# First block's mixers: norm chains on GpSimd, queries and keys without the row scale, one reciprocal for two softmaxes, two kinds of copies on ScalarE

## The chip, the cores and the metric

The kernel runs on one core of a Trainium2 chip. The metric is the device time of one execution in microseconds, the median of several executions. Engine names are short throughout: PE is TensorE, DVE is VectorE, ACT is ScalarE, POOL is GpSimd, SP is SyncE.

## What is computed

Two transformer blocks of two layers each, run one after the other on 512 tokens of width 1024, all in float32. The change touches only the mixer of the first block. There 16 meta tokens are put in front, so the sequence has 528 rows. Cut to what matters:

```python
for l in range(DEPTH):                       # DEPTH = 2
    hn = rms_norm(h, norm_mix_g[l])
    proj = hn @ w_in[l]                      # 1024 -> 2560
    q, k, v, xr, gate = jnp.split(proj, splits, axis=-1)
    q = apply_partial_rope(rms_norm(q, q_norm_g[l]), cos, sin)   # per head of 64
    k = apply_partial_rope(rms_norm(k, k_norm_g[l]), cos, sin)
    o_attn = diff_attention(q, k, v, lam)    # softmax(q1 k1) - lam softmax(q2 k2), times v
    o_attn = rms_norm(o_attn, subln_g[l]) * (1.0 - lam_init)     # per head of 128
    o_rec = rms_norm(rg_lru_branch(xr, gate, ...), rec_norm_g[l])  # over 512
    h = h + jnp.concatenate([o_attn, o_rec], axis=-1) @ w_out[l]
    ...                                      # norm, gated feed-forward of 2816
```

`rms_norm(x, g)` is `x * rsqrt(mean(x * x) + 1e-6) * g`.

## The kernel before

Features lie on partitions, tokens on the free dimension. Each product with a weight is done three times on PE (`mm3`, L95 to L98: high part times high part, high times low, low times high), in spans of 264 columns (two spans of 264 make 528) or, where the 16 meta rows are no longer needed, of 512. A weight tile is loaded by DMA, its high part is made by ACT (L90), its low part by DVE (L92); three of each can be in flight.

The first block's mixer runs per layer through a list of steps: the recurrent branch of four feature tiles (`r`), keys, queries and values of four head pairs (`k`, `q`, `v`), attention of a pair in two groups of rows (`a`), the gates (`g`), their norm (`R`, L545) and two passes of the output product (`w`). This list is only a priority. A scheduler of the framework lays the instructions of each engine down in a fixed order when the program is built, and interleaves the steps by what it takes each instruction to cost. On the chip every engine then works through its own order, and waits at the first instruction whose input is not there.

The norms all go through `rnorm` (L153). PE sums the squares over partitions with matmuls of two columns (L161, tile `av`). DVE turns the sums into mean plus epsilon (L164, tile `nwv`), and `rsqrt` (L128) makes 1/sqrt in eight dependent instructions on tiles of 88 x 12 or 128 x 8 numbers (L135 to L148, tiles `nwy`, `nwt`, `nwu`). For queries and keys, ACT then widens the result (L170, tile `nrep`); for the other norms PE reads it directly. PE transposes it into a PSUM bank (L176, tile `bc`), and DVE multiplies the data by it (L399 for queries and keys, L518 for the attention's output). In the text a **chain** is the part from L164 to L148.

In the two mixers there are 26 such chains outside the norms of the residual: 16 for queries and keys (`rows`, L389), 8 for the attention's output (end of `attend1`, L516), 2 for the recurrent branch (`recout`, L548).

Queries and keys come out of PSUM with a multiplication by `rbc`, the row scale of the preceding norm (L396, DVE, 28 instructions). The softmaxes of the two halves of a differential head each have a reciprocal (L489, 72 in all). The attention's output is copied from PSUM by DVE (L513, 16 instructions) and squared by ACT (L514).

Of the kernel before, what the change touches and what calls it, by code (L numbers as in the profile page):

```python
# [9 lines left out]
F32 = mybir.dt.float32  # L10
F32R = mybir.dt.float32r
BF = mybir.dt.bfloat16
I32 = mybir.dt.int32
AF = mybir.ActivationFunctionType
OP = mybir.AluOpType
AX = mybir.AxisListType

D = 1024
S = 512
NM = 16  # L20
T = S + NM
# [4 lines left out]
# columns of the first block's packed per-feature parameters  # L26
G_MIX, G_FFN, QG, KG, SUB, CW, CB, BRG, BIG, LRU, RECG, LAM = 0, 8, 16, 17, 18, 19, 35, 39, 43, 47, 51, 55
N_PAR1 = 59
# columns of the packed shape constants
# [5 lines left out]
# columns of the second block's packed per-feature parameters  # L35
# [11 lines left out]
def both_blocks(ctx: ExitStack, tc: tile.TileContext, xT, cst, par1, w1in, w1out, w1gu, w1dn, wgate,  # L47
# [6 lines left out]
    EARLY = 4  # tiles of features that the norms' first centre is taken from  # L54
# [7 lines left out]
    # ---- residual (features on partitions) and constants  # L62
# [4 lines left out]
    # the operand of most products: 8 tiles in two parts each  # L67
# [14 lines left out]
    # ---- building blocks  # L82
# [23 lines left out]
    def share(part):  # L106
        """who has the extra bank in a part of the program"""
        nonlocal extra
        extra = EXTRA[part]
# [18 lines left out]
    def rsqrt(pool, v, rows, n, between=()):  # L128
        """1/sqrt: y from half the exponent, then y (1 + a polynomial of v y^2 - 1) to the last bit"""
# [5 lines left out]
        nc.vector.tensor_scalar(y.bitcast(I32), v.bitcast(I32), -0.5, 1597463007.0, op0=OP.mult, op1=OP.add)  # L135
        next(other, None)
        nc.vector.tensor_mul(t, y, y)
        next(other, None)
        nc.vector.tensor_mul(t, t, v)
        next(other, None)  # L140
        nc.vector.tensor_scalar(t, t, -1.0, RSQRT[0], op0=OP.add, op1=OP.mult)
        next(other, None)
        nc.vector.scalar_tensor_tensor(u, t, RSQRT[1], t, op0=OP.add, op1=OP.mult)
        for c in RSQRT[2:]:
            next(other, None)
            nc.vector.scalar_tensor_tensor(u, u, c, t, op0=OP.add, op1=OP.mult)
        next(other, None)
        nc.vector.scalar_tensor_tensor(y, u, 1.0, y, op0=OP.add, op1=OP.mult)  # L148
# [4 lines left out]
    def rnorm(pool, xs, a, b, rhs, n, eps):  # L153
        """1/sqrt(the sums of xs over the partitions, as rhs groups them, / n + eps), on every partition of a group"""
        c = rhs.shape[1]
# [7 lines left out]
        v = pool.tile([128, 16], F32, name="nwv", bufs=3)  # L163
        nc.vector.tensor_scalar(v[:ch, :2 * J], ps[:ch, :2 * J], 1.0 / n, eps, op0=OP.mult, op1=OP.add)  # L164
        y = rsqrt(pool, v, ch, 2 * J)
# [25 lines left out]
    def tables():  # L191
        """rope tables of the given positions"""
# [27 lines left out]
    # ================= first block  # L220
    WOUT = ((0, 4), (4, 8))  # what the mixer's output product sums over, group by group
    # weights of the second block's mixer whose low parts GpSimd makes
    POOLW = (1, 0, 1, 0, 1, 0, 1)
    # tiles of the output product over half the tokens at a time, at its end and its start
    MIXTAIL = 3
    MIXHEAD = 0
    # steps whose weights are scaled by VectorE
    BYDVE = ('A010', 'A201', 'A211')
    # the first input products of the second block's mixer
    HEAD = (2, 3, 0)  # L230
    # pairs of tiles that a norm writes as one
    MERGED = (2, 4)
    # the order of the tiles of queries for the choice of keys
    TOPK = (2, 3, 1)
    # the order of the second block's mixer: H I Q input products, i scores of the indexer, p a part of the choice of
    # keys, d attention to the chosen ones, C and A attention in chunks (pair, head, group of rows), v convolution
    STEPS2 = ('H', 'I', 'Q0', 'i2', 'Q2', 'i1', 'i3', 'Q1', 'C0', 'd0', 'A000', 'A001', 'C1', 'A011', 'A100', 'A010', 'A101', 'p', 'A110', 'A111', 'C2', 'v0', 'p', 'd3', 'p', 'p', 'A201', 'p', 'd2', 'v1', 'A200', 'p', 'd1', 'A211', 'p', 'A210')
    # the order of the first block's mixer: r recurrent branch, k q v of a head pair, a attention (pair, group of rows),
    # g gates, R their norm, w output product
# [3 lines left out]
    for l in range(2):  # L243
# [4 lines left out]
        with ExitStack() as lay:  # L248
# [76 lines left out]
            with ExitStack() as mixer:  # L325
# [63 lines left out]
                def rows(m, gain, spans, dst):  # L389
# [5 lines left out]
                    for p, a, b in proj(w, xa, spans):  # L395
                        nc.vector.tensor_mul(raw[:, a:b], p, rbc[:, a:b])  # L396
# [826 lines left out]
```

## Time and profile before

| | |
|---|---|
| device time, median of 3 executions | 2865.7 us (2865.55 to 2867.1) |
| profiled execution, first to last instruction | 2861.2 us |
| PE busy in it | 2781.5 us, 97% |
| DVE / ACT / POOL busy | 1736.3 / 1227.4 / 367.0 us |
| stretches of the two mixers | about 30 to 255 us and 660 to 890 us |

The profiled execution's span, 2861.2 us, is what the rows further down are parts of. It is 4.5 us under the median of the three times, a share that lies around the span and is taken as constant. Matmuls are pipelined, so that PE counts as busy while one is in flight: busy time close to 100% means that no gap is longer than the pipeline, not that no time is lost.

### The profile page before, as it was taken

What the parts mean: (1) busy time and instruction counts of PE and PEld (TensorE: products, weight loads), DVE (VectorE), ACT (ScalarE), POOL (GpSimd) and SP (SyncE); (2) the same over time, 40 slices, a digit from 0 to 9 for tenths busy, and PEclk for the clock granted to TensorE, in tenths of its full rate; (3) what the DMA queues carried; (4) which work ended last, traced back from release to release, by engine and by line L of the source; (5) the groups of instructions that cost most, each with busy time, mean ns of one, the idle gap of its engine ahead of it and who ended that gap; (6) DMA issues with size and microseconds to landing.
All of it is one profiled execution on the core that took longest, in us unless ns stands there. A gap on an engine that the chain in (4) does not pass through costs nothing.

```text
span 2861.2 us, 42993 instructions
## 1 busy us (share of the span) xinstructions
PE 2781.5 (97%) x16548; PEld 2422.5 (85%) x16548; DVE 1736.3 (61%) x3534; ACT 1227.4 (43%) x2174; POOL 367.0 (13%) x403
## 2 busy tenths in 40 slices
PE   8989999999999999999999999999999999999998
PEld 7989999999887888887889888888877898888887
DVE  7887434457888434458977573333789875633335
ACT  6665222235665222235665442332445754433323
POOL 0011000000110000002220031111322110311112
PEclk9999999999999999999999999999999999999999
DMA  4332332332333333336324123333264242233331
GB/s 146 89 79 85 90 89 85 94 89 92 99 85 100 95 92 94 94 95 166 112 82 140 59 81 97 96 96 96 70 155 132 75 136 72 60 106 95 96 96 64
DMA packets 96491, 277.18 MB, mean 97 GB/s; under 512 B 13344, under 2 KB 20000, under 8 KB 96288
## 3 DMA queue, kind: packets, MB, share of 16 engines
q1 hardware_dynamic: 96288, 274.45, 32.7%
q8 instruction: 131, 2.15, 0.3%
q14 instruction: 72, 0.59, 0.1%
HBM read 241.82 MB, written 2.10 MB: 85 GB/s over the span
## 4 chain that ended last, share of the span: by engine, by line
PE 87%; DVE 8%; issue 2%; ACT 2%; POOL 1%; DMA 1%; SPq 0%; ACTq 0%; DVEq 0%; POOLq 0%
PE mm L97 25%; PE mm L98 25%; PE mm L96 25%; PE av L96 1%; PE av L97 1%; PE av L98 1%; PE av L161 1%; DVE wlo L92 1%; PE bc L827 1%; PE av L712 1%; PE tr L827 1%; DVE sq L402 1%; PE bc L176 0%; PE sc L96 0%; PE sc L833 0%
## 5 line engine op out<-in xcount | busy, mean ns | idle before, releaser
L96 PE MATMUL mm<-xh_all,whi 128*128 128x512 f32 (+2 forms) x2752 | 926.0, 338 | 12.4 <-ACT xh_all L260 6.8
L97 PE MATMUL mm<-xl_all,whi 128*128 128x512 f32 (+2 forms) x2752 | 930.3, 339 | 1.4 <-DVE xl_all L745 0.8
L98 PE MATMUL mm<-xh_all,wlo 128*128 128x512 f32 (+2 forms) x2752 | 925.9, 337 | 0.0
L90 ACT CAST whi<-wraw 128x1024 fp32r<-128x1024 f32 (+2 forms) x460 | 465.4, 1013 | 1017.7 <-PE mm L97 823.9
L92 DVE TENSOR_TENSOR wlo<-wraw,whi 128x1024 fp32r<-128x1024 f32 (+2 forms) x437 | 540.7, 1238 | 233.7 <-ACT whi L90 231.7
L96 PEld LDWEIGHTS mm<-xh_all,whi 128*128 128x128 f32 x2752 | 518.8, 189 | 66.6 <-ACT xh_all L260 6.8
L97 PEld LDWEIGHTS mm<-xl_all,whi 128*128 128x128 f32 x2752 | 519.8, 189 | 54.5 <-DVE xl_all L745 1.8
L98 PEld LDWEIGHTS mm<-xh_all,wlo 128*128 128x128 f32 x2752 | 521.0, 189 | 49.8
L1106 POOL TENSOR_TENSOR r<-r 128x512 f32<-128x512 f32 (+1 forms) x70 | 101.9, 1456 | 531.6 <-ACT r L1105 531.6
L97 PE MATMUL mm<-yl,whi 128*128 128x264 f32 (+1 forms) x528 | 169.9, 322 | 0.1
L98 PE MATMUL mm<-yh,wlo 128*128 128x264 f32 (+1 forms) x528 | 169.5, 322 | 0.0
L96 PE MATMUL mm<-yh,whi 128*128 128x264 f32 (+1 forms) x528 | 168.5, 320 | 0.0
L673 DVE TENSOR_TENSOR hall<-hall,mm 128x512 f32<-128x512 f32 (+1 forms) x82 | 46.6, 568 | 145.9 <-PE mm L98 145.9
L593 DVE TENSOR_TENSOR su<-mm,rbc 128x264 f32<-128x264 f32 (+1 forms) x66 | 34.3, 519 | 139.8 <-PE mm L98 139.8
L602 DVE TENSOR_TENSOR hall<-hall,mm 128x264 f32<-128x264 f32 (+1 forms) x72 | 37.1, 515 | 120.6 <-PE mm L98 120.6
L97 PEld LDWEIGHTS mm<-yl,whi 128*128 128x128 f32 x528 | 99.2, 188 | 8.8 <-DVE yl L122 0.6
L96 PEld LDWEIGHTS mm<-yh,whi 128*128 128x128 f32 x528 | 99.0, 188 | 7.6
L98 PEld LDWEIGHTS mm<-yh,wlo 128*128 128x128 f32 x528 | 99.2, 188 | 7.3
L588 DVE TENSOR_TENSOR sg<-mm,rbc 128x264 f32<-128x264 f32 (+1 forms) x66 | 34.0, 517 | 103.2 <-PE mm L98 101.6
L671 DVE SCALAR_TENSOR_TENSOR hall<-hall,mm 128x512 f32<-128x512 f32 x32 | 22.0, 687 | 66.9 <-PE mm L98 66.8
L692 POOL TENSOR_TENSOR accq<-accq,nsq 128x512 f32<-128x512 f32 (+1 forms) x48 | 57.9, 1205 | 25.4 <-ACT nsq L690 24.0
L432 POOL MEMSET vh<- 128x128 f32 x8 | 1.6, 205 | 463.6 <-PE mm L98 414.8
(672 smaller groups left out, 5446.3 us busy)
## 6 DMA issues: line engine op xcount, KB each, us to landing
wraw<-w2f SPq DMA_DIRECT2D x128, 512.0 KB, 3.7
wraw<-w1gu SPq DMA_DIRECT2D x88, 512.0 KB, 3.6
wraw<-w2in SPq DMA_DIRECT2D x44, 512.0 KB, 3.9
wraw<-w1in SPq DMA_DIRECT2D x40, 512.0 KB, 3.7
wraw<-w2mkv SPq DMA_DIRECT2D x32, 512.0 KB, 3.8
wraw<-w1dn SPq DMA_DIRECT2D x32, 448.0 KB, 3.3
wraw<-w1out SPq DMA_DIRECT2D x32, 256.0 KB, 2.7
wraw<-w1dn SPq DMA_DIRECT2D x16, 512.0 KB, 3.5
```

The source lines that it names most:

```text
L90: nc.scalar.copy(hi[:, :kt], raw[:, :kt])
L92: (eng or nc.vector).tensor_sub(lo[:, :kt], raw[:, :kt], f(hi[:, :kt]))
L96: nc.tensor.matmul(ps, wh, xh, start=first, stop=False)
L97: nc.tensor.matmul(ps, wh, xl, start=False, stop=False)
L98: nc.tensor.matmul(ps, wl, xh, start=False, stop=last)
L588: nc.vector.tensor_mul(sg[:, a:b], p, r2[:, a:b])
L593: nc.vector.tensor_mul(su[:, a:b], p, r2[:, a:b])
L602: nc.vector.tensor_add(h[m][:, a:b], h[m][:, a:b], p)
L673: nc.vector.tensor_add(X(m, a, b), X(m, a, b), p)
L692: nc.gpsimd.tensor_add(self.accq[:, a:b], self.accq[:, a:b], sq[:, a:b])
L827: nc.tensor.transpose(ps[:, 128 * j:128 * j + 128], p[:, 128 * j:128 * j + 128], ident)
L1106: nc.gpsimd.tensor_mul(r[:, a:b], r[:, a:b], r[:, a:b])
```

## The change

It makes five edits, all in the mixers of the first block.

1. `rsqrt` and `rnorm` take an engine. The chains of queries and keys, of the attention's output and of the recurrent norm go to POOL. [...] The first instruction (mean plus epsilon, out of PSUM) stays with DVE.
2. Queries and keys are no longer multiplied by the row scale. The norm takes the scale out anyway, if epsilon is multiplied by the mean square of the row, which `rnorm` of the preceding norm now keeps (`kept`, tile `ms`). L164 becomes a scalar_tensor_tensor there. In the second layer, four extra matmuls and two DVE instructions make `msl`, the same numbers in the token grouping that the queries use; each layer has one more DVE instruction to scale `ms`.
3. With that, the copy of queries and keys out of PSUM is a plain copy, by ACT.
4. The reciprocals of the two halves are one instruction over a stepped pair of columns.
5. The copy of the attention's output out of PSUM goes from DVE to ACT.

```diff
-    def rsqrt(pool, v, rows, n, between=()):
+    def rsqrt(pool, v, rows, n, between=(), eng=None):
+        eng = eng or nc.vector
...
-        nc.vector.scalar_tensor_tensor(u, t, RSQRT[1], t, op0=OP.add, op1=OP.mult)
+        if eng is nc.gpsimd:
+            for n, c in enumerate((*RSQRT[1:], 1.0)):
+                eng.tensor_scalar(u, u if n else t, c, None, op0=OP.add)
+                eng.tensor_mul(u if c != 1.0 else y, u, t if c != 1.0 else y)
+            return y
+        eng.scalar_tensor_tensor(u, t, RSQRT[1], t, op0=OP.add, op1=OP.mult)
...
-    def rnorm(pool, xs, a, b, rhs, n, eps):
+    def rnorm(pool, xs, a, b, rhs, n, eps, eng=None, scales=None, kept=None):
...
-        v = pool.tile([128, 16], F32, name="nwv", bufs=3)
-        nc.vector.tensor_scalar(v[:ch, :2 * J], ps[:ch, :2 * J], 1.0 / n, eps, op0=OP.mult, op1=OP.add)
-        y = rsqrt(pool, v, ch, 2 * J)
+        v = pool.tile([128, 16], F32, name="nwv", bufs=3) if kept is None else kept
+        if scales is None:
+            nc.vector.tensor_scalar(v[:ch, :2 * J], ps[:ch, :2 * J], 1.0 / n, eps, op0=OP.mult, op1=OP.add)
+        else:
+            nc.vector.scalar_tensor_tensor(v[:ch, :2 * J], ps[:ch, :2 * J], 1.0 / n, scales[:ch, :2 * J], op0=OP.mult,
+                                           op1=OP.add)
+        y = rsqrt(pool, v, ch, 2 * J, eng=eng)
...
-                rows = rnorm(small, sumsq(small, h, 0, T), 0, T, one2, D, 1e-6)
+                ss = sumsq(small, h, 0, T)
+                rows = rnorm(small, ss, 0, T, one2, D, 1e-6, kept=ms)
+                ps = bank("av")
+                for j in range(4):
+                    nc.tensor.matmul(ps[:, 2 * j:2 * j + 2], ss[0][:, l0 + 128 * j:l0 + 128 * j + 128], one2, start=True, stop=True)
+                nc.vector.tensor_scalar(msl[:, :8], ps[:, :8], 1.0 / D, 1e-6, op0=OP.mult, op1=OP.add)
+                nc.vector.tensor_scalar(msl[:, :8], msl[:, :8], 1e-6, None, op0=OP.mult)
...
+            nc.vector.tensor_scalar(ms[:88, :12], ms[:88, :12], 1e-6, None, op0=OP.mult)
...
                     for p, a, b in proj(w, xa, spans):
-                        nc.vector.tensor_mul(raw[:, a:b], p, rbc[:, a:b])
+                        nc.scalar.copy(raw[:, a:b], p)
                     nc.scalar.activation(sq[:, a0:b0], raw[:, a0:b0], AF.Square)
-                    for p, a, b in rnorm(small, [sq], a0, b0, blk, 64, 1e-6):
+                    for p, a, b in rnorm(small, [sq], a0, b0, blk, 64, 1e-6, nc.gpsimd, ms if a0 == 0 else msl):
...
-                            nc.vector.reciprocal(st[:n, o + 5:o + 6], st[:n, o + 3:o + 4])
                             pr.append(p)
+                        nc.vector.reciprocal(st[:n, 5:12:6], st[:n, 3:10:6])
...
-                    nc.vector.tensor_copy(oT[:, g0:g1], ps[:, :g])
+                    nc.scalar.copy(oT[:, g0:g1], ps[:, :g])
...
-                    for p, a, b in rnorm(small, [sq], l0, T, one2, 128, 1e-6):
+                    for p, a, b in rnorm(small, [sq], l0, T, one2, 128, 1e-6, nc.gpsimd):
...
-                    for p, a, b in rnorm(small, sums, l0, T, one2, 512, 1e-6):
+                    for p, a, b in rnorm(small, sums, l0, T, one2, 512, 1e-6, nc.gpsimd):
```

The scheduler lays the two mixers down anew on every engine; from the second block on, all five orders are as before. Two places show what moves. The names carry buffer numbers here, which differ between the programs; the line numbers of the changed program are larger by 5 to 18.

First, DVE in layer 0 at the norm of the first queries (sums `av_784` before, `av_789` after). `d` and `xc` belong to the recurrent branch, `raw_943` to the next keys. Before:

```order
L164 TENSOR_SCALAR nwv_791<-av_784 88x12
L378 TENSOR_SCALAR d_711<-d_711 128x528
L135 TENSOR_SCALAR nwy_793<-nwv_791 88x12
L356 SCALAR_TENSOR_TENSOR xc_888<-xr_834,par_81,xc_888 128x528
L137 TENSOR_TENSOR nwt_794<-nwy_793 88x12
L396 TENSOR_TENSOR raw_943<-mm_945,rbc_174 128x264
L139 TENSOR_TENSOR nwt_794<-nwt_794,nwv_791 88x12
L356 SCALAR_TENSOR_TENSOR xc_888<-xr_834,par_81,xc_888 128x528
L141 TENSOR_SCALAR nwt_794<-nwt_794 88x12
L92 TENSOR_TENSOR wlo_1156<-wraw_1152,whi_1154 128x1024
L381 TENSOR_TENSOR d_711<-d_711,ig_689 128x528
L143 SCALAR_TENSOR_TENSOR nwu_795<-nwt_794 88x12
```

After:

```order
L172 SCALAR_TENSOR_TENSOR nwv_796<-av_789,ms_115 88x12
L374 SCALAR_TENSOR_TENSOR xc_684<-xr_630,par_81,xc_684 128x528
L370 TENSOR_TENSOR xr_843<-mm_845,rbc_174 128x264
L122 TENSOR_TENSOR xcl_690<-xc_684,xch_689 128x528
L417 SCALAR_TENSOR_TENSOR raw_734<-raw_734,gs_186,bc_815 128x264
L370 TENSOR_TENSOR xr_843<-mm_870,rbc_174 128x264
L417 SCALAR_TENSOR_TENSOR raw_734<-raw_734,gs_186,bc_819 128x264
```

Before, the chain's steps stand between the recurrent branch's and a weight's, and `raw` times `bc` (L399) comes 21 instructions after L164. After, three instructions stand between L172 and the multiplication that needs the broadcast (L417). On PE at the same place, 69 matmuls of 264 columns stood between the sums and the first broadcast of this norm; now 30 do.

Second, PE in layer 0 at the recurrent branch's norm (`R`), from the sums to the first broadcast. `mm` is the gates' product, `sc` the scores of an attention tile. Before:

```order
L161 MATMUL av_2615<-one2_74,ss_acc_2130 88x2 x6
L97 MATMUL mm_3038<-rl3_2608,whi_3034 128x264
L98 MATMUL mm_3038<-rh3_2607,wlo_3036 128x264
L471 MATMUL sc_2678<-k1_1447,qs_1558 128x272
L476 MATMUL sc_2678<-k2_1448,qs_1558 128x272
L471 MATMUL sc_2682<-k1_1447,qs_1558 128x256
L474 LDWEIGHTS ident_b_76
L474 MATMUL sc_2682<-mask_b_77,ident_b_76 128x128
L476 MATMUL sc_2682<-k2_1448,qs_1558 128x256
L176 MATMUL bc_2635<-cs_68,nwy_2624 128x88 x3
```

After:

```order
L166 MATMUL av_2643<-one2_74,ss_acc_2157 88x2 x6
L98 MATMUL mm_3046<-rh3_2635,wlo_3031 128x264
L97 MATMUL mm_3071<-rl3_2636,whi_3067 128x264
L98 MATMUL mm_3071<-rh3_2635,wlo_3069 128x264
L489 MATMUL sc_2723<-k1_1463,qs_1578 128x272
L185 MATMUL bc_2667<-cs_68,nwy_2652 128x88 x3
```

Eight matmuls between sums and broadcast have become four.

## Rows read from the trace of the kernel before

**Rows 1.** The page: busy time of the engines; the chain that ended last.
```profile
PE 2781.5 (97%) x16548; PEld 2422.5 (85%) x16548; DVE 1736.3 (61%) x3534; ACT 1227.4 (43%) x2174; POOL 367.0 (13%) x403
...
PE 87%; DVE 8%; issue 2%; ACT 2%; POOL 1%; DMA 1%; SPq 0%; ACTq 0%; DVEq 0%; POOLq 0%
```

**Rows 2.** Windows: length, busy us (instructions) of each engine, clock, DMA.
```profile
30.00:255.00 225.00, 212.04 (x1694) 197.37 (x1692) 185.10 (x502) 137.40 (x275) 32.20 (x51) 0.98 0.28 77
660.00:890.00 230.00, 221.12 (x1472) 191.62 (x1472) 194.91 (x487) 138.15 (x265) 31.50 (x47) 1.00 0.31 84
300.00:350.00 50.00, 50.00 (x413) 50.00 (x412) 24.05 (x36) 14.13 (x18) 0.00 (x0) 1.00 0.30 87
950.00:1000.00 50.00, 50.00 (x218) 40.53 (x217) 22.07 (x26) 14.07 (x17) 0.00 (x0) 1.00 0.34 96
```

**Rows 3.** PE's waits, 30 to 255 us: total us, times, longest.
```profile
PE sc L471 <- ACT p L485: 3.1, 1, 3.1
PE av L161 <- ACT sq L397: 2.2, 4, 0.8
PE bc L176 <- DVE nwy L148: 2.0, 2, 1.4
```

**Rows 4.** Groups by shape, DVE: count, busy us, mean ns, idle before.
```profile
L396 DVE TENSOR_TENSOR raw<-mm,rbc 128x264 f32<-128x264 f32 x24 | 10.0, 419 | 0.5 <-PE mm L98 0.5
L489 DVE RECIPROCAL st<-st 128x1 f32<-128x1 f32 x64 | 9.6, 155 | 2.5 <-ACT p L485 2.1
L513 DVE COPY oT<-av 128x256 f32<-128x256 f32 x12 | 5.1, 421 | 4.4 <-PE av L98 4.3
L137 DVE TENSOR_TENSOR nwt<-nwy 88x12 f32<-88x12 f32 x20 | 3.2, 160 | 0.2
```

**Rows 5.** Groups by shape, ACT, 0 to 950 us.
```profile
L170 ACT COPY nrep<-nwy 88x768 f32<-88x768 f32 x12 | 9.9, 826 | 4.0 <-DVE nwy L148 4.0
L288 ACT COPY rbc<-bc 128x264 f32<-128x264 f32 x4 | 1.5, 378 | 6.5 <-PE bc L176 6.5
```

**Rows 6.** Timeline (start, length): a chain alone on DVE, then PE's broadcast.
```profile
248.57 0.17 DVE L164 TENSOR_SCALAR nwv<-av 88x12 f32<-88x12 f32 x1 [0.75 <-PE av L161]
...
250.19 0.17 DVE L148 SCALAR_TENSOR_TENSOR nwy<-nwu,nwy 88x12 f32<-88x12 f32 x1
250.41 0.44 PE L176 MATMUL bc<-cs,nwy 88*128 88x88 f32 x3
```

**Rows 7.** Timeline: the first queries' chain among other work; widening; broadcast.
```profile
72.50 0.17 DVE L164 TENSOR_SCALAR nwv<-av 88x12 f32<-88x12 f32 x1 [0.38 <-PE av L161]
...
79.92 0.83 ACT L170 COPY nrep<-nwy 88x768 f32<-88x768 f32 x1 [1.71 <-DVE nwy L148]
...
80.84 0.33 PE L176 MATMUL bc<-cs,nrep 88*128 88x88 f32 x2
```

**Rows 8.** POOL: groups by shape, then timeline rows, undisturbed.
```profile
L350 POOL MEMSET xr<- 128x3 f32 x8 | 0.8, 100 | 53.1 <-DVE xc L356 31.6 <-PE av L161 19.2 <-PE av L98 1.9
...
200.41 1.31 POOL L401 TENSOR_TENSOR raw<-raw,ct 128x528 f32<-128x528 f32 x1 [4.54 <-DVE sq L400]
208.62 0.74 POOL L559 TENSOR_TENSOR hall<-hall,raw 128x264 f32<-128x264 f32 x1 [6.90 <-DVE raw L558]
...
1493.11 1.31 POOL L692 TENSOR_TENSOR accq<-accq,nsq 128x512 f32<-128x512 f32 x1 [4.29 <-ACT nsq L690]
1494.49 1.29 POOL L692 TENSOR_TENSOR accq<-accq,nsq 128x512 f32<-128x512 f32 x1
...
1500.26 0.74 POOL L692 TENSOR_TENSOR accq<-accq,nsq 128x256 f32<-128x256 f32 x1
1500.95 0.73 POOL L682 TENSOR_TENSOR acc<-acc,hall 128x256 f32<-128x256 f32 x1
```

**Rows 9.** Timeline: POOL and DVE at the same time.
```profile
247.13 0.69 DVE L92 TENSOR_TENSOR wlo<-wraw,whi 128x512 fp32r<-128x512 f32 x1
247.20 1.22 POOL L559 TENSOR_TENSOR hall<-hall,raw 128x264 f32<-128x264 f32 x1 [0.72 <-DVE raw L558]
```

More of the change, by code (lines that the diff above doesn't have):

```diff
@@ L134, in rsqrt @@
         other = iter(between)
-        nc.vector.tensor_scalar(y.bitcast(I32), v.bitcast(I32), -0.5, 1597463007.0, op0=OP.mult, op1=OP.add)
+        eng.tensor_scalar(y.bitcast(I32), v.bitcast(I32), -0.5, 1597463007.0, op0=OP.mult, op1=OP.add)
         next(other, None)
-        nc.vector.tensor_mul(t, y, y)
+        eng.tensor_mul(t, y, y)
         next(other, None)
-        nc.vector.tensor_mul(t, t, v)
+        eng.tensor_mul(t, t, v)
         next(other, None)
-        nc.vector.tensor_scalar(t, t, -1.0, RSQRT[0], op0=OP.add, op1=OP.mult)
+        eng.tensor_scalar(t, t, -1.0, RSQRT[0], op0=OP.add, op1=OP.mult)
         next(other, None)
-        nc.vector.scalar_tensor_tensor(u, t, RSQRT[1], t, op0=OP.add, op1=OP.mult)
+        if eng is nc.gpsimd:
[4 more added lines that the diff above has]
+        eng.scalar_tensor_tensor(u, t, RSQRT[1], t, op0=OP.add, op1=OP.mult)
         for c in RSQRT[2:]:
             next(other, None)
-            nc.vector.scalar_tensor_tensor(u, u, c, t, op0=OP.add, op1=OP.mult)
+            eng.scalar_tensor_tensor(u, u, c, t, op0=OP.add, op1=OP.mult)
         next(other, None)
-        nc.vector.scalar_tensor_tensor(y, u, 1.0, y, op0=OP.add, op1=OP.mult)
+        eng.scalar_tensor_tensor(y, u, 1.0, y, op0=OP.add, op1=OP.mult)
         for _ in other:
@@ L151, in rsqrt @@
         return y
-    def rnorm(pool, xs, a, b, rhs, n, eps):
-        c = rhs.shape[1]
+    def rnorm(pool, xs, a, b, rhs, n, eps, eng=None, scales=None, kept=None):
         ch = 88 if (b - a) % 88 == 0 else 128
@@ L271, in both_blocks @@
             prep(G_MIX, 0, T)
+            ms = small.tile([128, 16], F32)
+            msl = small.tile([128, 16], F32, name="msl") if l else ms
             if l == 0:
@@ L282, in both_blocks @@
                             nc.vector.tensor_add(acc, acc, sq)
-                    rows = rnorm(small, [acc], 0, T, one2, D, 1e-6)
+                    rows = rnorm(small, [acc], 0, T, one2, D, 1e-6, kept=ms)
             else:
-                rows = rnorm(small, sumsq(small, h, 0, T), 0, T, one2, D, 1e-6)
+                ss = sumsq(small, h, 0, T)
[5 more added lines that the diff above has]
+                nc.vector.tensor_scalar(msl[:, :8], msl[:, :8], 1e-6, None, op0=OP.mult)
             rbc = small.tile([128, T], F32, name="rbc", bufs=1)
```

## The prediction

> **What bounds the kernel now.** I read the page's busy times and chain first. PE is busy 97% of the span, and it is 87% of the chain that ended last [rows 1]. So an edit counts only by what it does to PE: work taken off DVE is worth nothing in itself. Second come the windows, to see what each stretch is limited by. In the feed-forward stretches PE has no gap, and 413 matmuls of 264 columns go through in 50 us, 0.121 us each; in layer 1, with 512 columns, it is 218, or 0.229 us each [rows 2]. These are the prices of a matmul below. In the two mixers PE is busy 212.0 of 225 us and 221.1 of 230 us, so it idles 13.0 and 8.9 us, 21.9 us in all. DVE is busy 185 and 195 us there, 82% and 85%, ACT about 60%, POOL 14% [rows 2]. That is the pool the change can draw from: if every gap of PE in both mixers went away, the time would fall by 21.9 us, 0.8%, and no further.
>
> Third, what ends PE's gaps. In layer 0 the largest are one of 3.1 us for an exponential, 2.2 us in four pieces for the squares of queries and keys, and 2.0 us in two pieces for the end of a norm's chain [rows 3]. The first and the last stand together at the recurrent norm. The rest is spread thin, mostly on DVE and ACT being late by less than a microsecond. A general relief of DVE can shorten such gaps. But a matmul order that is fixed beforehand has its own demand: whatever stands between the sums of a norm and its broadcast must last as long as the norm's chain, or PE waits at the broadcast. I call that work the **cover**.
>
> **The change part by part.**
>
> *DVE and ACT.* DVE loses 26 chains of eight steps at 0.20 us (nine instructions take 1.79 us when alone [rows 6]), 42 us; 28 multiplications at 0.42, 12 us; 36 of 72 reciprocals at 0.155, 6 us; 16 copies at 0.42, 7 us [rows 4]. It gains five small instructions, 1 us. That is 66 us of the 380 it is busy in the mixers. ACT gains 28 + 16 copies out of PSUM at 0.38 [rows 5], 17 us on 276: the buffers of queries and keys are freed through ACT now, with about the same duration as by DVE. The four extra matmuls of layer 1 are under 1 us. All this is off PE's path and counts only through the 21.9 us above.
>
> *The chain on POOL.* No row shows POOL with tiles of 12 columns, so I bound a step by others. Two tensors of 264 columns take 0.74 us and of 528 columns 1.31 us [rows 8]: 2.2 ns per column and 0.17 us fixed, so 0.20 us at 12 columns. The steps depend on one another. Of two dependent POOL instructions, the second began 0.07 us after the first had ended (1493.11 + 1.31 = 1494.42, then 1494.49); of two independent ones, 0.05 us before (1500.26 + 0.74 = 1501.00, then 1500.95) [rows 8]. So a step costs 0.28 us and twelve of them 3.4 us, where DVE's eight needed 1.6 us alone. Six of the twelve have one tensor only; the shortest POOL instruction in the trace, a memset of three columns, takes 0.10 us [rows 8], which bounds the chain from below at 6 x 0.28 + 6 x 0.18 = 2.8 us. From above, POOL and DVE hinder each other: 264 columns took 1.22 us instead of 0.74 beside a DVE subtraction of two SBUF tiles, ending 0.60 us after it [rows 9], so POOL stood until DVE was done. In the new DVE order one to three such instructions of about 0.7 us stand between the start of a chain and the point where DVE itself waits for the broadcast. I charge one wait of 0.35 us and take **3.7 us** for the chain.
>
> The Trainium skill, GPSIMD Engine Reference, section Engine selection, speaks against this edit: elementwise add and multiply belong on VectorE, since GpSimd is about 2x slower with two inputs. By that factor on DVE's 0.16 us [rows 4] a chain would be, as an estimate, 12 x 0.33 = 4.0 us, and the sum below 8 us more; the rows give a fixed part that is closer to DVE's, so I stay with them.
>
> *Cover against need.* Around the chain come DVE's first instruction (0.17 us) and three hand-overs of about 0.04 us [rows 6]: a norm of the attention's output or of the recurrent branch needs 3.7 + 0.3 = 4.0 us from sums to broadcast. Queries and keys need another 0.83 us for ACT's widening and 0.1 us of hand-overs [rows 7], 4.9 us. For the cover I counted, in the order of both programs, the matmuls between sums and first broadcast of every chain, at the prices above. Before: 6.0 us on average for the 16 of queries and keys, 3.4 us for the other ten. The first queries' norm is an example: 69 matmuls, 8.4 us, over a chain that began at 72.50 with its broadcast at 80.84, 8.3 us later [rows 7]. After: **3.4 us** and **1.9 us** (the same norm 30 matmuls, 3.6 us; the recurrent norm of layer 0 four matmuls, 0.5 us). The scheduler has evidently taken a POOL step for about half of what I find. So PE waits 4.9 - 3.4 = 1.5 us at 16 places, 24 us, and 4.0 - 1.9 = 2.1 us at ten, 21 us. Nothing covers this: PE goes in order, the broadcast stands next, and DVE waits at the multiplication behind it with the recurrent branch's work queued after that. One more place: the norm that opens layer 1 stays with DVE, but its cover falls from 16 instructions to 5, 0.4 us, against 1.8 us for its chain [rows 6], 1.4 us.
>
> *What comes back.* When PE arrives later, the small waits on DVE and ACT end before it comes, and DVE has less to do. I let all of the 21.9 us go except some 4 us at the recurrent norm of layer 0, where the new wait takes the old one's place: 18 us back. The floor is about 10 us, if the waits for ACT's squares, exponentials and casts stay.
>
> **Sum**: 24 + 21 + 1.4 - 18 = +28 us. The profiled span of 2861.2 us becomes 2889.6, and with the 4.5 us that lie between the span and the median, 2865.7 becomes **2894 us**. Each 0.1 us of chain is worth 26 x 0.1 = 2.6 us; the sum crosses zero at a chain of 2.6 us, or 0.22 us per step.
>
> **The rivals.**
>
> *The chain fits its cover* (not slower). If a step costs what the memset costs, 0.10 us and some 0.04 us of hand-over, the chain is 1.7 us, the needs are 2.0 and 2.9 us, and the covers of 1.9 and 3.4 us hold. Then only the relief is left; half of the 21.9 us, 11 us, against 2 us of new waits gives 2857 us. It decides from a chain under 2.6 us. For it: the scheduler's order assumes it. Against it: memsets read nothing, and both two-tensor slopes leave 0.17 us.
>
> *It cancels* (no change). With the lower bound of 2.8 us the needs are 3.1 and 4.0 us, the waits 10 x 1.2 + 16 x 0.6 = 22 us, and with all 21.9 us given back the time is 2867 us.
>
> *The port decides* (much slower). If each POOL step meets a DVE instruction with two SBUF inputs and waits for it as in [rows 9], a chain is 5 us or more, the waits 10 x 3.4 + 16 x 2.8 = 79 us, and the time about 2928 us. Against it: DVE soon stands at the broadcast itself and leaves POOL alone. The Trainium skill, SBUF — State Buffer, section Who interferes with whom, has this as a rule: a VectorE instruction with two SBUF inputs contends with a GpSimd instruction that reads SBUF, and the pair of ports is an exclusive lock; rows 9 agree with it, 1.22 us for 0.74.
>
> **How the numbers follow.** The forecast, 2894 us with a range of its own of 2876 to 2912 (chains of 3.0 to 4.4 us), gets 0.54; the fitting chain 0.15; the cancelling 0.14; the port 0.17. The range of 8 in 10 goes from 2858 to 2922: it leaves out half of the fitting chain's cases and a bit over half of the port's. A measurement of this kernel can tell about 0.2%, 5.7 us, from no change: faster (under 2860) has 0.14, nearly all of the fitting chain; same 0.14; slower 0.72.
>
> **What would show it.** In the changed profile the mixers should be longer by some 15 us each, with the feed-forward stretches and the second block as before. PE's waits should name the broadcast (now L185) behind POOL's last step or ACT's widening as the largest item, some 40 us, where L176 had 2.0 us. POOL's steps should take about 0.2 us with 0.07 us between them, some 3.7 us per chain, and DVE's busy time in the mixers should fall by about 60 us with no gain from it. Steps of 0.1 us, or broadcasts that PE reaches after POOL is done, would show the forecast wrong; so would PE waits that stay where they were.

## The result, and the profile after

The changed kernel takes 2941.15 us (median of 4 executions, 2937.27 to 2942.44) against 2865.62 us of the kernel before. That is 75.5 us more: the two medians divided give 1.0264, the ratio on record is 1.0255 with a 95% interval of 1.0241 to 1.027. The kernel got slower, where the prediction had 28 us more and ended its range at 2922 us. The direction was right, the size was not.

The page of the changed kernel, busy times and the chain that ended last, against [rows 1]:

```profile
PE 2812.4 (96%) x16556; PEld 2451.3 (83%) x16556; DVE 1700.9 (58%) x3250; ACT 1242.1 (42%) x2218; POOL 446.9 (15%) x715
...
PE 84%; DVE 7%; POOL 3%; issue 2%; ACT 2%; DMA 0%; SPq 0%; ACTq 0%; DVEq 0%; POOLq 0%
```

PE has only eight instructions more, but is busy 31 us longer. This is the first sign that waiting alone doesn't explain the result: the same matmuls took longer. POOL's share of the chain rose from 1% to 3%.

The windows of the changed kernel (length, busy us of PE, PEld, DVE, ACT, POOL, then the granted clock) show where. The first two rows are the mixers, the third is the feed-forward stretch of layer 0; the others are pieces of 25 us inside the mixers:

```profile
30.00:310.00 280.00, 248.22 (x1907) 233.33 (x1906) 190.58 (x398) 160.61 (x322) 71.89 (x207) 0.95 0.27 75
690.00:985.00 295.00, 257.01 (x1560) 220.91 (x1560) 203.59 (x412) 166.50 (x317) 71.17 (x203) 0.94 0.28 77
310.00:690.00 380.00, 379.93 (x3114) 379.15 (x3113) 165.07 (x250) 97.62 (x115) 0.00 (x0) 1.00 0.30 91
...
30.00:55.00 25.00, 24.65 (x200) 23.74 (x199) 18.28 (x29) 16.89 (x27) 1.97 (x8) 1.00 0.20 64
55.00:80.00 25.00, 18.91 (x136) 18.29 (x135) 15.09 (x25) 11.62 (x17) 9.03 (x23) 0.87 0.34 86
80.00:105.00 25.00, 21.98 (x162) 21.35 (x161) 17.55 (x27) 16.81 (x27) 6.88 (x17) 0.86 0.28 74
...
690.00:715.00 25.00, 19.10 (x125) 17.86 (x125) 18.81 (x67) 14.10 (x25) 0.67 (x5) 0.80 0.21 65
```

PE idles 280 - 248.2 = 31.8 us and 295 - 257.0 = 38.0 us, together 69.8 us, where it idled 13.0 and 8.9 us before [rows 2]. That is 47.9 us more. (These windows are longer than those of rows 2; what they hold besides the mixers is feed-forward work, in which PE has no gap.) Besides, the clock has fallen in both mixers. It is at one of two levels, 1.2 or 2.4 GHz, so a mean of 0.87 over 25 us is 6.5 us at 1.2 GHz. Summed over the 25 us pieces, the mixers spend 30.5 and 34 us at 1.2 GHz. Before it was 7 us, all in this piece of the first mixer:

```profile
200.00:225.00 25.00, 20.36 (x141) 17.31 (x141) 19.61 (x62) 12.14 (x37) 6.56 (x9) 0.86 0.32 87
```

At the lower level a matmul takes at most twice as long (0.22 us for 0.12 in the rows of the seam below), so 57.5 us more of it cost at most 28.8 us. The two sums, 47.9 and at most 28.8, make up to 76.7 us. ACT's last cast for layer 1's feed-forward begins at 977.5 us for 901.7 before, so 75.8 us are lost by the end of the second mixer, of the 77.3 by which the two profiled spans differ. The feed-forward stretch of layer 0 is as before.

PE's waits in the two mixers (total us, times, longest), layer 0 and then layer 1:

```profile
PE bc L185 <- ACT nrep L179: 13.9, 7, 3.2
PE bc L185 <- POOL nwy L147: 10.2, 5, 2.4
PE tr L518 <- DVE p L511: 3.8, 7, 0.9
PE av L166 <- ACT sq L415: 1.5, 2, 0.9
PE sc L489 <- ACT p L503: 1.2, 1, 1.2
...
PE bc L185 <- ACT nrep L179: 17.6, 8, 3.0
PE bc L185 <- POOL nwy L147: 9.6, 5, 3.0
PE mm L96 <- ACT xh_all L269: 3.3, 1, 3.3
PE av L166 <- ACT sq L415: 1.7, 2, 1.1
PE tr L518 <- DVE p L511: 1.7, 3, 1.1
PE bc L185 <- DVE nwy L154: 1.3, 1, 1.3
```

At the broadcasts (L185), POOL's last step and ACT's widening hold PE for 13.9 + 10.2 + 17.6 + 9.6 = 51.3 us in 25 waits. Those behind ACT are at queries and keys (31.5 us in 15 waits), those behind POOL at the other norms (19.8 us in 10). These are the waits that the prediction named. The 3.3 us for `xh_all` are new, and stand where it did not look.

**POOL's steps.** POOL has 715 - 403 = 312 instructions more than before, 12 for each of the 26 chains. The timeline of a chain that DVE leaves alone, and of one that it doesn't (start, length):

```profile
143.96 0.68 DVE L122 TENSOR_TENSOR vl<-tr,vh 128x512 fp32r<-128x512 f32 x1
144.05 0.20 POOL L138 TENSOR_TENSOR nwt<-nwy 88x12 f32<-88x12 f32 x1
...
144.34 0.21 POOL L140 TENSOR_TENSOR nwt<-nwt,nwv 88x12 f32<-88x12 f32 x1
...
144.63 0.20 POOL L142 TENSOR_SCALAR nwt<-nwt 88x12 f32<-88x12 f32 x1
```

```profile
52.83 0.69 DVE L394 SCALAR_TENSOR_TENSOR d<-rg,d 128x528 f32<-128x528 f32 x1
...
52.99 0.59 POOL L136 TENSOR_SCALAR nwy<-nwv 88x12 int32<-88x12 int32 x1 [8.99 <-DVE nwv L172]
...
55.40 1.30 POOL L147 TENSOR_TENSOR nwu<-nwu,nwt 88x12 f32<-88x12 f32 x1
55.40 1.22 DVE L92 TENSOR_TENSOR wlo<-wraw,whi 128x1024 fp32r<-128x1024 f32 x1 [0.19 <-ACT whi L90]
```

Undisturbed, a step takes 0.20 or 0.21 us here (0.24 us at most in this chain) and the next begins 0.08 to 0.09 us after it; the DVE instruction that runs beside these steps has one of its inputs, `tr`, in PSUM. Beside a DVE instruction with two SBUF inputs, the same kind of step takes 0.59 or 1.30 us and ends 0.06 or 0.08 us after that instruction. Over the 16 groups of steps in the first 1000 us, the 26 chains are busy 81.9 us with 23.0 us of gaps, 4.03 us per chain. The rule that the prediction cited from the Trainium skill (SBUF — State Buffer, Who interferes with whom) fits these rows, but such steps are few. Undisturbed, a chain would take 12 x 0.21 + 11 x 0.085 = 3.5 us, so they make some 0.5 us of it, where the prediction had charged 0.35 and the rival that built on them over 1.6 (5 us or more, for 3.4 without them).

**The seam between the layers.** PE at the end of layer 0, and the loads of layer 1's parameters by SP in the changed kernel and in the kernel before:

```profile
692.01 0.28 PE L98 MATMUL mm<-yh,wlo 128*128 128x264 f32 x1
695.54 1.03 PE L96 MATMUL mm<-xh_all,whi 128*128 128x264 f32 x3 [3.25 <-ACT xh_all L269]
...
697.28 0.42 PE L96 MATMUL mm<-xh_all,whi 128*128 128x264 f32 x1
697.50 0.42 PE L97 MATMUL mm<-xl_all,whi 128*128 128x264 f32 x1
...
702.55 0.29 PE L96 MATMUL mm<-xh_all,whi 128*128 128x264 f32 x1
702.67 0.28 PE L98 MATMUL mm<-xh_all,wlo 128*128 128x264 f32 x1
```

```profile
692.37 0.33 SPq L260 DMA_DIRECT2D par<-par  x1
```

```profile
622.15 0.33 SPq L251 DMA_DIRECT2D par<-par  x1
```

Before, the parameters (`par`, with the gain that scales layer 1's input) were loaded 40 us before layer 0's last down product ended, and ACT scaled and cast each residual tile as it became ready, while PE still multiplied. Now the load begins when the last down product is over. All eight casts come after it, and PE waits 3.25 us. Then matmuls follow each other by 0.22 us for some 6 us, until they are back at 0.12 us. The window of the first of them shows the clock at the lower level:

```profile
695.00:700.00 5.00, 4.35 (x18) 4.04 (x19) 5.00 (x11) 5.00 (x9) 0.00 (x0) 0.50 0.35 108
```

### The profile page after: what moved, and what is told of

It is laid out like the page before. It is cut to its first block, busy times and chain, and to the rows that moved or that the text cites. A ratio compares the mean times of both kernels' runs of the same rounds, so it can differ in the third digit from the quotient of the medians.

```text
span 2938.5 us, 43082 instructions
## 1 busy us (share of the span) xinstructions
PE 2812.4 (96%) x16556; PEld 2451.3 (83%) x16556; DVE 1700.9 (58%) x3250; ACT 1242.1 (42%) x2218; POOL 446.9 (15%) x715
## 4 chain that ended last, share of the span: by engine, by line
PE 84%; DVE 7%; POOL 3%; issue 2%; ACT 2%; DMA 0%; SPq 0%; ACTq 0%; DVEq 0%; POOLq 0%
PE mm L97 25%; PE mm L98 25%; PE mm L96 25%; PE av L96 1%; DVE wlo L92 1%; PE av L97 1%; POOL nwu L146 1%; PE av L98 1%; PE av L166 1%; PE bc L185 1%; POOL nwu L147 1%; PE bc L845 1%; PE av L730 1%; PE tr L845 1%; PE sc L96 0%
## 5 line engine op out<-in xcount | busy, mean ns | idle before, releaser
L96 PEld LDWEIGHTS mm<-xh_all,whi 128*128 128x128 f32 x2752 | 526.5, 192 | 70.5 <-ACT xh_all L269 10.1
L97 PEld LDWEIGHTS mm<-xl_all,whi 128*128 128x128 f32 x2752 | 527.3, 192 | 54.9 <-DVE xl_all L270 1.6
L98 PEld LDWEIGHTS mm<-xh_all,wlo 128*128 128x128 f32 x2752 | 528.4, 192 | 49.9
L92 POOL TENSOR_TENSOR wlo<-wraw,whi 128x1024 fp32r<-128x1024 f32 x23 | 55.9, 2429 | 36.3 <-ACT whi L90 35.3
```

The lines of the kernel that those rows point to most:

```text
L92: (eng or nc.vector).tensor_sub(lo[:, :kt], raw[:, :kt], f(hi[:, :kt]))
L96: nc.tensor.matmul(ps, wh, xh, start=first, stop=False)
L97: nc.tensor.matmul(ps, wh, xl, start=False, stop=False)
L98: nc.tensor.matmul(ps, wl, xh, start=False, stop=last)
```

## The experiments

The theory after these readings: three things make the 75 us, waits at the broadcasts, 1.2 GHz behind waits, and the seam. The rivals: POOL's work itself costs, by the port or by the clock, wherever it stands; or edits 2 to 5 have a cost of their own. The kernel before was timed again beside each group of runs (2864.8 to 2866.2 us).

**e1_even: layer 1's pool no larger than layer 0's.**

```diff
-            msl = small.tile([128, 16], F32, name="msl") if l else ms
+            msl = small.tile([128, 16], F32, name="msl")
```

> The changed kernel with one difference: the tile of 64 bytes a partition that only layer 1 had (msl) is allocated in both layers, so that layer 1's pool of small tiles is no larger than layer 0's. In the built order the load of layer 1's parameters then stands before the last three down weights again, not behind six input weights. Theory (three terms: waits at the broadcasts, half clock after waits, and a seam between the layers): the seam goes, PE's 3.3 us wait for xh_all and the half-clock stretches at 695 to 718 us with it, 8 to 14 us less, 2927 to 2933 us. Rival (the chains on POOL cost everything, the seam only shows what is late anyway): 2941 us, within 4.

Measured: 2926.58 us, 14.6 less than the changed kernel. The wait for `xh_all` is gone; the waits at the broadcasts are 50.0 us, nearly what they were. That layer 1 alone had this tile of 64 bytes a partition cost 14.6 us.

**e2_even_dve: without edit 1.**

```diff
-... rnorm(small, [sq], a0, b0, blk, 64, 1e-6, nc.gpsimd, ms if a0 == 0 else msl):
+... rnorm(small, [sq], a0, b0, blk, 64, 1e-6, None, ms if a0 == 0 else msl):
-... rnorm(small, [sq], l0, T, one2, 128, 1e-6, nc.gpsimd):
+... rnorm(small, [sq], l0, T, one2, 128, 1e-6):
-... rnorm(small, sums, l0, T, one2, 512, 1e-6, nc.gpsimd):
+... rnorm(small, sums, l0, T, one2, 512, 1e-6):
```

> As e1, and the 26 chains are back on DVE: edits 2 to 5 without edit 1. Theory (the waits at the broadcasts and the half clock behind them come from the chains on POOL): both terms go, 2848 to 2868 us, and PE waits at the broadcasts for less than 10 us in both mixers. Rival (the copies moved to ACT and the new order are a cause of their own): 2885 us or more.

Measured: 2868.13 us (2860.48 to 2871.3), a ratio to before of 1.0009 (1.0 to 1.0019). So edit 1 carries 58.5 us and edits 2 to 5 nothing that can be told. The windows of both mixers, first of e2 (an execution of 2860.48 us, the shortest of its ten), then of the kernel before in the same stretches:

```profile
30.00:320.00 290.00, 280.86 (x2253) 266.17 (x2252) 215.92 (x532) 171.17 (x338) 32.32 (x51) 0.99 0.30 85
650.00:980.00 330.00, 321.10 (x1936) 273.46 (x1935) 249.07 (x543) 187.23 (x342) 28.43 (x47) 1.00 0.32 91
```

```profile
30.00:320.00 290.00, 277.01 (x2230) 262.14 (x2229) 226.61 (x576) 166.52 (x315) 32.20 (x51) 0.99 0.30 83
650.00:980.00 330.00, 321.12 (x1948) 274.74 (x1947) 256.30 (x577) 181.42 (x321) 31.50 (x47) 1.00 0.33 93
```

DVE is relieved of 18 us here, and PE gains 3.9 us in one mixer and nothing in the other, in e2's shortest execution. The longest waits that are left are for scores' exponentials and attention tiles (L503, L511), 4.5 us each in both mixers, where the kernel before had 3.9 and 4.8: the relief doesn't shorten them.

**e3_chains_only: edit 1 alone, on the kernel before.**

```diff
-    def rnorm(pool, xs, a, b, rhs, n, eps):
+    def rnorm(pool, xs, a, b, rhs, n, eps, eng=None):
...
-        y = rsqrt(pool, v, ch, 2 * J)
+        y = rsqrt(pool, v, ch, 2 * J, eng=eng)
...
-                    for p, a, b in rnorm(small, sums, l0, T, one2, 512, 1e-6):
+                    for p, a, b in rnorm(small, sums, l0, T, one2, 512, 1e-6, nc.gpsimd):
```

> The kernel before, and the 26 chains on POOL with its twelve steps: edit 1 without edits 2 to 5. There is no msl here, and the load of layer 1's parameters stands before the down weights. Theory (chains on POOL): waits at the broadcasts and half clock as in the changed kernel without its seam, 2915 to 2940 us. Rival (edits 2 to 5 carry a good part): under 2895 us.

Measured: 2923.21 us, 58.4 more than before. With e2, both halves agree: edit 1 costs the same with edits 2 to 5 or without them.

**e4_fill: work for nothing between sums and broadcast.**

```diff
             ps = bank("bc")
+            if eng is nc.gpsimd and j0 == 0:
+                for _ in range(FILL):
+                    nc.tensor.matmul(ps[:, :96], xs[0][:, a:a + 128], xs[0][:, a:a + 96], start=True, stop=True)
```

> As e1, and between the sums of each of the 26 norms and its broadcast PE does eight matmuls of 96 columns into the broadcast's bank, whose result the broadcast overwrites: work for nothing, which adds nothing to the output. Theory (the half clock follows PE's waits and costs some 19 us outside the seam): the waits get shorter by what the fill takes, fewer stretches are at 1.2 GHz (under 25 us in both mixers for 51), and the time is 5 to 20 us below e1 although PE does more. Rival (the clock has no part): the fill at best lies in the waits, the time is that of e1 or up to 20 us above.

Measured: 2967.4 us, 41 more than e1: both missed. The waits at the broadcasts fell only from 50 to 37 us, while PE was busy 50.6 us longer (2854.4 for 2803.8), so most of the fill did not lie in the waits; the mixers' clock stayed where it was (0.95 and 0.97). It decides nothing about the clock; e10 and e11 do more.

**e5_shadow: POOL does the chains too, and nobody waits for it.**

```diff
-        y = rsqrt(pool, v, ch, 2 * J, eng=eng)
+        if eng is not None:
+            rsqrt(pool, v, ch, 2 * J, eng=eng, idle="i")
+        y = rsqrt(pool, v, ch, 2 * J)
```

> As e2 (chains on DVE, edits 2 to 5 kept, equal pools), and POOL does its 26 chains of twelve steps as well, from the same sums, into tiles that nobody reads. So POOL has the work of the changed kernel, and no engine waits for it. Theory (PE's clock falls because PE waits at the broadcasts): the time of e2, 2868 us, plus at most 10 us for steps that DVE and POOL hinder each other in; the half clock in the mixers stays at 7 us as in e2. Rival (POOL's work itself, by the port that it shares with DVE or by the clock, makes the mixers longer): 2890 us or more, with the clock under 0.97 in the mixers.

Measured: 2876.14 us, 8 more than e2, with waits for attention tiles of up to 2.9 us in layer 0. POOL is busy as in the changed kernel:

```profile
30.00:320.00 290.00, 274.07 (x2183) 260.39 (x2182) 214.85 (x528) 172.09 (x337) 81.95 (x207) 0.97 0.29 82
650.00:980.00 330.00, 320.79 (x1959) 275.72 (x1958) 249.78 (x546) 187.43 (x342) 72.60 (x203) 0.99 0.32 93
```

So POOL's work beside DVE's costs some 8 us, where e2's ten executions alone span 11. The other 50 of edit 1's 58 come only when the broadcasts wait for it. The clock in layer 0 is 0.97 for 0.99 in e2's window, but that is e2's shortest execution; over the whole program, e5's five executions have 0.988 to 0.990 and e2's ten 0.989 to 0.995. That the clock stays at e2's level was too much to expect.

**e6_late: the same chains, the broadcast written behind the next step.**

```diff
-                    for p, a, b in rnorm(small, [sq], a0, b0, blk, 64, 1e-6, nc.gpsimd, ms if a0 == 0 else msl):
+                    rest = rnorm(small, [sq], a0, b0, blk, 64, 1e-6, nc.gpsimd, ms if a0 == 0 else msl, later=True)
+                    yield
+                    sq = at.tile([128, T], F32, name="sq", bufs=1)
+                    for p, a, b in rest():
```

> As e1 (chains on POOL), but each of the norms gives up its turn between the chain and the broadcast: the broadcast and what follows it are written behind the next step of the list. By the order, PE has 4.6 us of matmuls between sums and broadcast of queries and keys (3.3 in e1) and 3.5 us at the other norms (1.9 in e1), unevenly. Theory (cover against need, with the needs that e1 shows, 5.1 and 3.9 us): the waits at the broadcasts fall from 50 to about 28 us, the half clock with them, 2890 to 2905 us. Rival (POOL's steps cost by themselves wherever the broadcast stands): 2920 us or more.

Measured: 2930.38 us, a miss, and a time that the rival allows; but e5 has POOL's steps without the waits, and they cost 8 us there. The waits at the broadcasts fell from 50.0 to 35.0 us. Some are now of another kind (7.3 us for DVE's multiplication by the broadcast before, which holds the one bank). The clock took it all back:

```profile
30.00:320.00 290.00, 263.83 (x2008) 245.71 (x2007) 195.40 (x408) 162.96 (x328) 77.25 (x207) 0.93 0.28 76
650.00:980.00 330.00, 300.73 (x1885) 263.76 (x1884) 225.23 (x457) 180.39 (x332) 69.40 (x203) 0.93 0.30 83
```

0.93 over 620 us is 87 us at 1.2 GHz, where e1's windows (0.95 over 290 us, 0.97 over 320 us) have 48. In the whole program PE idles 10.0 us less than in e1 and is busy 12.4 us longer (2816.2 for 2803.8).

**e7_seam: the kernel before, with one unused tile of 64 bytes in layer 1.**

```diff
             prep(G_MIX, 0, T)
+            if l == 1:
+                nc.vector.memset(small.tile([128, 16], F32, name="more"), 0.0)
```

> The kernel before with one addition: a tile of 64 bytes a partition that layer 1 alone allocates in its pool of small tiles, set to zero once and read by nobody. In the built order the load of layer 1's parameters moves from before the last three down weights to behind six input weights. Theory (the seam comes from the pool that grew from layer 0 to layer 1): 2865 us plus what the changed kernel lost there, 2876 to 2882 us, with a PE wait for xh_all of about 3 us and half clock behind it. Rival (a tile more costs nothing, the seam needs the other edits): 2865 us, within 4.

Measured: 2889.18 us, 23 more than before. PE's wait at the seam is there, without any other edit:

```profile
PE mm L96 <- ACT xh_all L260: 3.2, 1, 3.2
```

The seam is a cause of its own. It was priced too low: the clock in 650 to 980 us is 0.96 here, for 1.00 before, so it also fell later in that mixer.

**e8_qk_only: only the 16 chains of queries and keys on POOL.** The edit is that of e2 without its first change.

> As e1, with the chains of queries and keys alone on POOL (16); those of the attention's output and of the recurrent branch (10) stay on DVE. Theory: the 16 places carry their waits, 30 us in e1, and a like share of the half clock, so about 0.6 of the way from e2 (2868 us) to e1 (2927 us), 2898 to 2910 us. Rival (the recurrent branch's and the attention's norms, with the smallest cover, carry nearly all): under 2885 us.

Measured: 2905.01 us, 37 above e2, or 63% of the way to e1. PE waits 11.3 + 13.3 = 24.6 us behind the widening. Both kinds of norm carry their share.

**e9_ffn_dve, e10_ffn_pool, e11_ffn_pool3: the price of a wait by itself.** 22 chains that nobody reads go into the stretch where PE has no gap: on DVE, on POOL, and on POOL three times in a row.

```diff
                         nc.vector.tensor_mul(su[:, l0:], su[:, l0:], sg[:, l0:])
+                        if l == 0:
+                            rnorm(small, [su], 0, T, one2, 1.0, 1e6, nc.gpsimd)
```

> The kernel before with 22 chains put into the feed-forward stretch of layer 0, where PE has no gap: after each product of gate and up, the sums of a tile, the norm's chain on DVE, the broadcast, read by nobody. In the built order 28 matmuls of 264 columns (3.4 us) stand between sums and broadcast. This run gives the price of the added matmuls alone, since a chain on DVE (about 2 us) fits: 2866 us plus 15 to 30 us, no PE waits at the broadcasts, no half clock between 280 and 700 us. Rival (a chain costs wherever it is put): PE waits at the broadcasts here too, over 1 us each.

> As e9, with those 22 chains on POOL, all else on DVE as in the kernel before. The order now has 21 matmuls (2.6 us) between sums and broadcast, though the chain is longer. Theory (wait = need - cover): need 4.0 us, a wait of 1.4 us at 22 places, 31 us above e9, and more than that only by half clock behind the waits. Rival (steps on POOL are slow in the mixers only by what DVE does there): under 15 us above e9.

> As e10, each chain three times in a row (36 steps on POOL): 43 matmuls (5.2 us) of cover against a need of about 11 us, a wait of some 5.5 us at 22 places, in the same surroundings. Theory (a long wait lowers the clock and costs more than its length): the stretch shows the clock at 1.2 GHz behind the waits, and the time is 130 us or more above e10, where the waits alone make 90 us. Rival (the clock has nothing to do with PE's waits): 80 to 100 us above e10, clock 1.00 in the stretch.

Measured: 2908.79, 2964.71 and 3117.83 us. The window from 280 to 890 us, which holds all the chains and in e9 and e10 part of layer 1's mixer, of e9, then of e10 and e11, each followed by its largest group of PE's waits:

```profile
280.00:890.00 610.00, 603.31 (x4772) 573.14 (x4771) 362.44 (x881) 221.25 (x339) 18.67 (x35) 1.00 0.29 85
```

```profile
280.00:890.00 610.00, 570.19 (x4475) 546.86 (x4474) 294.38 (x591) 191.31 (x282) 77.48 (x290) 0.97 0.26 78
```

```profile
PE bc L182 <- POOL nwy L147: 36.7, 22, 1.8
```

```profile
280.00:890.00 610.00, 451.03 (x3323) 440.09 (x3323) 162.33 (x276) 95.74 (x116) 198.39 (x792) 0.83 0.17 52
```

```profile
PE bc L184 <- POOL nwy L147: 158.6, 22, 7.3
```

The start of ACT's last cast for layer 1's feed-forward (the second of the two times before the shapes) shows how far each is behind at the end of the second mixer:

```profile
L266 ACT ACTIVATE xh_all<-hall,par x32: 709/732/740, 5.7 to 948.7; 128x528 fp32r<-128x528 f32 x24, 128x512 fp32r<-128x512 f32 x8
L266 ACT ACTIVATE xh_all<-hall,par x32: 710/728/740, 5.8 to 996.9; 128x528 fp32r<-128x528 f32 x24, 128x512 fp32r<-128x512 f32 x8
L268 ACT ACTIVATE xh_all<-hall,par x32: 707/732/740, 6.2 to 1156.6; 128x528 fp32r<-128x528 f32 x24, 128x512 fp32r<-128x512 f32 x8
```

e9: the added matmuls cost 44 us, more than the 15 to 30 I gave them, and PE waits 0.4 us at these broadcasts. e10: a wait at each of the 22 places, 1.67 us on average, where need minus cover (4.0 - 2.6) had given 1.4. By the cast e10 is 48.2 us behind e9, of which the waits are 36.3. e11: waits of 7.2 us each, where 5.5 had been expected: POOL's 792 instructions in the window take 0.25 us each, so that 36 of them with their gaps take some 12 us and not 11. By the cast e11 is 207.9 us behind e9, of which the waits are 158.2. The rest is 11.9 and 49.7 us. Some 3 us of each is the last matmul before a wait, for which PE counts as busy for 0.28 us where otherwise the next would begin after 0.12. What is left goes with the clock: 1.00 in e9, 0.97 in e10, 0.83 in e11, in a stretch where little else was changed. Behind a wait in e10, matmuls follow each other by 0.22 us:

```profile
480.03 0.44 PE L182 MATMUL bc<-cs,nwy 88*128 88x88 f32 x3 [1.67 <-POOL nwy L147]
...
481.38 0.42 PE L96 MATMUL mm<-xh_all,whi 128*128 128x264 f32 x1
481.60 0.42 PE L97 MATMUL mm<-xl_all,whi 128*128 128x264 f32 x1
```

So a wait of PE can cost more than its length. That POOL's work lowers the clock, and not PE's waits, doesn't fit e7, where the clock fell behind a wait with POOL's work as before. e10's whole span is 53.2 us over e9's (2960.6 and 2907.4); the 5.0 us beyond the 48.2 come later, behind the cast, where neither edit changes anything.

The page TensorE: Matmul & The Clock Gate of the Trainium skill says of TensorE's clock, in its section The HAM clock gate, that "the default state is throttled, and activity releases the throttle." The clocks of e9, e10 and e11 agree: 1.00, 0.97 and 0.83, the more PE waits.

The orders of e10 and e11 also show what the scheduler allows for a step on POOL. For 24 steps more it laid 22 matmuls more into the gap (21 and 43), at 0.121 us 2.7 us, or 0.11 us per step. An undisturbed step takes 0.29 us with its hand-over.

**e12_late_dve: e2 with the broadcasts written later.** The edit is that of e6, with the chains on DVE.

> As e2 (chains on DVE, edits 2 to 5), with the broadcasts written behind the next step as in e6: 6.0 us of cover for queries and keys and 4.6 for the others, more than in the kernel before. If a wait at a broadcast is still what holds e2, under 2860 us; if e2 has none left to give (1.9 us in both mixers), 2868 us within 8, or worse by what waits behind the one bank of the broadcasts, as e6 showed.

Measured: 2885.57 us, 17 more than e2, with 0.96 and 0.97 as the clock of the mixers for e2's 0.99 and 1.00. That it might get worse had been expected, but not in this way: behind the one bank PE waits little (3.4 us at all broadcasts, 1.9 in e2), while its waits for exponentials grew to 10.3 us, from 4.5. More cover than a chain needs buys nothing here. No version here beats the kernel before.

## Why the prediction was wrong in size and right in direction

The step that failed is the sum, 24 + 21 + 1.4 - 18. It took every matmul at its price at full clock, and so had no term for the clock; it took 18 us off for waits that would end, of which 8.5 came; and at the seam between the layers it put down only the 1.4 us of a norm. The waits at the broadcasts, its main term, were right.

- **The chain: right, a little short.** It was put at 3.7 us with steps of 0.2 us and 0.07 between; measured are 0.20 to 0.24 and 0.08 to 0.09, and 4.03 us on average. The two slopes of [rows 8] led to it from tiles over twenty times as wide. The 0.33 us more are worth some 9 us by the prediction's own 2.6 us for each 0.1 us. That the estimate of 4.0 us, which it worked out from a factor of 2 and set aside, comes nearer is luck: it put the factor on all twelve steps, of which half have one tensor only, and an undisturbed step takes 0.20 to 0.24 us and not 0.33; gaps and disturbed steps make up the rest.
- **Cover against need: right.** 24 + 21 + 1.4 = 46.4 us were forecast at the broadcasts. The trace has 51.3 us behind POOL and ACT, 1.3 us at the first norm of layer 1 and 0.5 us for the copy behind it, together 53.1. The excess is nearly all at queries and keys (31.5 us for 24; the other norms have 19.8 for 21). e8 bears out that both kinds of norm count, e9 and e10 the rule itself.
- **What comes back: wrong, 8.5 us of the 18 forecast.** PE's idle time is 69.8 us, of which the broadcasts are 53.1 and `xh_all` 3.3. So 13.4 us are left of the 21.9 that were there before: 8.5 came back, 2.0 of them at the broadcasts themselves [rows 3]. The error was to think that a later PE and a relieved DVE would end the small waits; the prediction's own floor of about 10 us was nearer. e2 gives the relief alone, without any new wait, and it is worth at most 3.9 us of PE's idle time and none of the median time.
- **The clock: a missing term, up to 28.8 us.** The rows [rows 2] had 0.98 in one mixer and 1.00 in the other, and the sum took every matmul at its full price. But the clock fell behind many of the new waits. This is the largest error. A hint stood in the rows that were read, 0.98 in the mixer with the longer waits and 1.00 in the stretches where PE had no gap; but the other mixer, with 8.9 us of gaps, had 1.00 too, so they gave no price.
- **The seam: a missing term, 14.6 us (e1), part of it again by the clock.** The prediction looked there at "the norm that opens layer 1" alone, 1.4 us. The new tiles were read as instructions, not as space, and SP's order, where the load of `par` had moved behind six input weights, was not looked at. That the 64 bytes were enough is shown by e1 and e7. Why is not shown: the likely reason is that layer 1's larger pool reaches into the space of the feed-forward tiles, which are in use until the last down product.
- **The port: right to leave it small.** e5 has POOL's work without the waits for it at 8 us.
- **DVE's relief: half, without effect.** DVE's busy time fell by 35.4 us in the whole program, not by 66. Steps were priced at 0.20 us each, but in the trace a DVE instruction can begin while the one before it still runs (L172 at 52.74 us for 0.17 us, then L394 at 52.83), so leaving one out saves less busy time than its length: e3, which takes the 208 steps of the chains off DVE and nothing else, saves 17.0 us (1719.3 for 1736.3), 0.08 us each. None of this was on PE's path.

In order: 28.4 us forecast, + 9.5 for what didn't come back, + 6.7 for longer waits at the broadcasts, + 3.3 for `xh_all` make the 47.9 us of idle time; the clock adds at most 28.8.

**What stays open.** Why one wait lowers the clock and the next doesn't: in e10 the clock was 1.00 from 300 to 450 us with waits of the same length as later. Why e6, with 15 us less of waiting at the broadcasts, spent more time at 1.2 GHz than e1. And why e10 loses 5.0 us to e9 behind the second mixer, where neither edit reaches. So the clock term can be read after the fact, but the runs give no price per wait. As an estimate, for each us of new waiting the rest was 0.3 us in e10 and e11 (11.9 for 36.3, 49.7 for 158.2) and up to 0.6 in the changed kernel (28.8 for 47.9); e6 fits neither.

## What to carry to other kernels

Where PE goes in a fixed order and is nearly always busy, moving a chain to a free engine is judged by the work that the order puts between its input and its reader, against the chain's length on the new engine; price the clock that falls behind the new waits as a term of its own. Freed time on an engine that PE rarely waits for is worth next to nothing, here at most 3.9 us of idle time for 18 us of work taken off it (e2). And a small new buffer in a pool that is opened once per layer can move a load: compare the order of the transfers too, not only that of the compute engines.

## What the runs showed of the hardware that was not expected

- With waits of 1.67 us, some 15 us apart, the clock fell in parts of a stretch that is otherwise full of matmuls (0.97 for 1.00, e10 and e9). With waits of 7.2 us it was 0.83 (e11).
- A POOL instruction with one tensor is held up by DVE as one with two is: 0.59 us for 0.20 beside a DVE instruction with two SBUF inputs (52.99 us). Nor does a narrow tile protect it: 12 columns took 1.30 us beside 1.22 us of DVE (55.40 us).
- Small DVE instructions between others cost less busy time than their length: 0.08 us for each of the 208 steps that e3 takes off DVE, where one takes 0.16 us by itself [rows 4].
